# Two modulation gates summed on TensorE's column groups, and a fourth weight slot beside the attention

## The chip, the cores and the metric

The kernel runs on one core of a Trainium2 chip. The metric is the time of one execution in device microseconds, taken as the median of several runs. One further execution is taken with the hardware profiler; its rows are what this document reads. The engines are named as in the profile: PE is TensorE (PEld its weight loads), DVE is VectorE, ACT is ScalarE, POOL is GpSimd, and SP is SyncE, which issues most of the transfers.

## The reference, cut to what matters

Two transformer blocks run over 256 tokens of width 1024. The change lies in the first one, in the part that computes the modulation and the two attentions:

```
mod = (jax.nn.silu(c) @ w_ada + b_ada)[:, None, :]
sh_mix, sc_mix, g_mix, sh_ffn, sc_ffn, g_ffn = jnp.split(mod, 6, -1)
...
tiny = tiny_attention(tq, tk, tv, tk_c, tv_c) @ tiny_w_o
o_a = spatial_gating(u, v, tiny, sgu_ln_g, sgu_ln_b, sgu_w_s, sgu_b_s)
o_b = neighbourhood_attention(nq, nk, nv, nk_c, nv_c, na_rpb, rows)

merged = gate_a * (o_a @ w_up_a) + gate_b * (o_b @ w_up_b)
x = x + g_mix * (merged @ w_out)
```

`w_ada` is 1024 x 6144. Its six column blocks give shifts, scales and the two gates `g_mix` (block 2) and `g_ffn` (block 5), each a row of 1024 numbers. The neighbourhood attention has 16 heads and 256 queries over 512 keys (256 of the image, 256 of the context). After this part a mixture of 64 experts follows, and then the second block.

## The kernel before

All matrix products with large weights are made in three passes: a weight tile of 128 x 2048 numbers arrives through a ring of buffers (`Ring`, its transfer issued by SP on line 222), ACT writes its rounded part `whi` (line 352), DVE the remainder `wlo` (line 353), and TensorE runs three matmuls for each block (lines 392 to 394 in the function `fm`, called fm matmuls below). There are two pairs of `whi` and `wlo`. The ring has three lasting slots; other pools lend it more in some stages. A slot is given back when `whi` and `wlo` of its tile are written, or, for a tile of `w_ada`, when its sums are made. SP issues its transfers strictly in its own order, so one that waits for a slot holds those behind it.

The stage of this document lies at 157 to 281 us of the profile. Its main work is eight weight tiles of the gates `gate_a` and `gate_b` (384 fm matmuls that read `hh`). Woven into it is background work: first `sgu`, eight groups of four fp32 matmuls (lines 1245, 1246 and 1248; they contract over 64 rows, 1 row and 128 rows), whose operands `two`, `bs` and `wst` sit in the tile `tw`. Then comes `na`, the neighbourhood attention: four groups of heads `g`, two halves of the queries `q`, and in each two pairs of heads, 16 pairs in all. For a pair TensorE makes the scores (line 1311), DVE adds the bias table `T` (line 1320) and takes the maximum (line 1262), ACT takes the exponential (line 1265), TensorE transposes (line 1278) and ACT copies the result into the tile `PT` (line 1279). After two pairs `av` follows: the reciprocals of the four sums, spread over 32 columns each (line 1335), a matmul that transposes them (line 1337), the product with the values in four column groups of 32 (line 1344), and its scaling.

The two gates ride along in the same stage. `ada_sums` gives each gate four steps of one `w_ada` tile; a step is two instructions of DVE over 128 x 1024 numbers (line 749), which add the tile's rows, weighted by the SiLU of `c`, into the tile `gate_row`. Here they are partial sums in all 128 partitions. `gate_bcast` adds them up and spreads them by a matmul with ones (line 778) and copies the result out (line 779). The first two blocks of `w_ada` go another way, through `ada_group`: there TensorE makes the sums (line 701), with the 32 columns of `silp` as stationary operand and the tile's four stretches of 256 columns in the four column groups of the array.

A scheduler lays down the order of each engine's instructions when the program is built; on the chip each engine keeps that order.

Of the kernel before, what the change touches and what calls it, by code (L numbers as in the profile page):

```python
# [9 lines left out]
F32 = mybir.dt.float32  # L10
# [4 lines left out]
OP = mybir.AluOpType  # L15
# [256 lines left out]
class Kernel:  # L272
# [454 lines left out]
    def ada_sums(self, g):  # L727

        nc = self.nc
        st = {}  # L730

        def step(n):
            if n == 0:

                st["a"] = self.gate_row[g if g == 2 else 5]
                if g == 5:
                    self.gate_init(5)
            a = st["a"]
            i = self.i_ada[4 * self.ADA_ORDER.index(g) + n]
            w = self.ring.get(i)[:].rearrange("p (k c) -> p k c", k=2)  # L740

            j = min((j for j in self.lo_of if j > i), default=None)
            with self.tc.issue_after(self.lo_of[j].ins) if j else ExitStack():
                for k in range(2):
                    c = self.silp[:, 2 * n + k, 0:1]
                    if n == 0 and k == 0 and g in (3, 4):
                        nc.vector.tensor_scalar(a[:], w[:, k], c, None, op0=OP.mult)
                    else:
                        nc.vector.scalar_tensor_tensor(a[:], w[:, k], c, a[:], op0=OP.mult, op1=OP.add)
            self.ring.done(i)  # L750

        def end():
            if g in (2, 5):
                return
            st["ps"] = self.accp.tile([128, 512], F32, tag="acc", name="acc")

        def col(k):
            ps, a = st["ps"], st["a"]
            nc.tensor.matmul(ps[:, k:k + 1], a[:, k * 128:(k + 1) * 128], self.ones[:, 0:1], start=k == 0, stop=k == 7,
                             skip_group_check=True)  # L760
            if k == 7:
                c0 = V_AD + (g - 3) * 8
                nc.vector.tensor_tensor(self.mod[:, g, :, 0], ps[:, 0:8], self.vecs[:, c0:c0 + 8], op=OP.add)

        return [lambda n=n: step(n) for n in range(4)] + [end] + ([] if g in (2, 5) else [lambda k=k: col(k) for k in range(8)])

    def gate_init(self, g):
# [14 lines left out]
    def block1(self):  # L782
        tc, nc, A = self.tc, self.nc, self.A
# [115 lines left out]
        bg = []  # L899
        late = []  # L900
        for g in self.ADA_ORDER[2:]:
            a = self.ada_sums(g)
            if g == 4:
                bg += [late + a[0:1], a[1:2], a[2:3], a[3:4]]
            else:
                bg += [a[0:1], late + a[1:2], a[2:3], a[3:4]]
            late = a[4:]
        ada = bg

        def along(n):  # L910
# [97 lines left out]
        op, o_es = self.pool("op")  # L1008
        self.dump("nv", nv[:])


        tmp, tmp_es = self.pool("atmp", "right", bufs=2)
        oah = op.tile([128, 8, 256], F32R, name="oah")
        oal = Parts()
        obh = op.tile([128, 4, 256], F32R, name="obh")
        obl = op.tile([128, 4, 256], F32R, name="obl")
        bg = self.sgu(tmp, tT, u, v, oah, oal)
# [11 lines left out]
        self.weave(main, bg)  # L1029
        self.dump("oa", oah[:].bitcast(F32))  # L1030
        self.dump("ob", obh[:].bitcast(F32))
        tmp_es.close()
        att_es.close()
        xp, xp_es = self.pool("xp", "right")
# [196 lines left out]

    def sgu(self, tmp, tT, u, vn, oah, oal):
        nc, A = self.nc, self.A
        big = tmp.tile([128, 2048], F32, tag="PT", name="tw")
        two, bs, wst = big[0:64, 0:1024], big[64:65, 0:1024], big[:, 1024:2048]
        nc.sync.dma_start(two, A["two"])
        nc.sync.dma_start(bs, A["bs"])
        nc.sync.dma_start(wst, A["wst"])
        ones1 = self.ones[64:65, :]

        def sgu(g):
            ps = self.accp.tile([128, 512], F32, tag="acc", name="acc")
            o = ps[:, 0:256]
            gs = slice(g * 128, (g + 1) * 128)
            nc.tensor.matmul(o, two[:, gs], tT[:], start=True, stop=False, skip_group_check=True)
            nc.tensor.matmul(o, ones1, bs[:, None, gs].to_broadcast([1, 2, 128]), start=False, stop=False, skip_group_check=True)
            for n in range(2):
                nc.tensor.matmul(ps[:, n * 128:(n + 1) * 128], vn[:, n, gs], wst[:, gs], start=False, stop=n == 1,
                                 skip_group_check=True)
            nc.vector.tensor_tensor(o, u[g][:], o, op=OP.mult)  # L1250
            u[g] = None
            lo = self.up.tile([128, 256], F32R, tag="u", name="oal", bufs=9)
            oal.parts.append(lo)
            self.split(o, oah[:, g], lo[:])

        return [lambda g=g: sgu(g) for g in range(8)]
# [24 lines left out]
    def na(self, ap, tmp, qd, kd, nv, obh, obl):  # L1281
        nc, A, c = self.nc, self.A, self.c
        st = {}
# [40 lines left out]

        def trp(g, q, j):
            if j == 0:
                st["PT", g, q] = tmp.tile([128, 4, 4, 128], F32, tag="PT", name="PT")
            self.transposeP(st.pop(("p", g, q, j)), st["PT", g, q][:, :, j, :], 4)

        def av(g, q):  # L1330
            PT = st.pop(("PT", g, q))
            r = st.pop(("r", g, q))
            ps = self.accp.tile([128, 512], F32, tag="acc", name="acc")
            rB = tmp.tile([128, 4, 32], F32, tag="obf", name="rB")
            nc.vector.reciprocal(rB[:], r[:, :, None].to_broadcast([128, 4, 32]))

            nc.tensor.matmul(ps[:, 128:256], rB[:].rearrange("p a b -> p (a b)"), self.ident, start=True, stop=False,
                             skip_group_check=True)
            o = tmp.tile([128, 128], F32, tag="obf", name="o")
            nc.scalar.copy(o[:], ps[:, 128:256])  # L1340
            for k in range(4):
                for j in range(4):
                    h = 4 * g + j
                    nc.tensor.matmul(ps[32 * j:32 * j + 32, 0:128], nv[:, k, h * 32:(h + 1) * 32], PT[:, k, j, :],
                                     start=False, stop=k == 3, tile_position=(0, 32 * j), skip_group_check=True)
            nc.vector.tensor_tensor(o[:], ps[:, 0:128], o[:], op=OP.mult)
            s = slice(q * 128, (q + 1) * 128)
            b = self.vecs[:, V_BNV + g:V_BNV + g + 1]
            nc.scalar.activation(obh[:, g, s], o[:], AF.Identity, bias=b)
            nc.vector.scalar_tensor_tensor(obl[:, g, s], o[:], b, obh[:, g, s].bitcast(F32), op0=OP.add, op1=OP.subtract)  # L1350
# [5 lines left out]
        for n in range(len(items) + 1):  # L1356
            if n < len(items):
                g, q, j = it = items[n]
                if q == 1 and j == 0 and g < 3:
                    out.append(lambda g=g: load(g + 1))  # L1360
                if q == 0 and j == 0 and 0 < g < 3:
                    out.append(lambda g=g: stack(g + 1))
                out.append(lambda it=it: score2(*it))
            if n:
                g, q, j = items[n - 1]
                for jj in (j, j + 2):
                    out.append(lambda p=(g, q, jj): trp(*p))
                if j:
                    out.append(lambda g=g, q=q: av(g, q))
# [1031 lines left out]
```

## Time and profile before

| | |
|---|---|
| median of 3 runs | 1612.58 us (1611.51 to 1612.89) |
| the profiled execution | 1612.77 us |
| its span, first to last instruction | 1611.0 us |
| mean granted TensorE clock | 0.99 of full speed |
| TensorE, VectorE, ScalarE busy | 97%, 55%, 39% of the span |
| the stage with attention and gates | 157.55 to 281.24 us, 123.69 us |

The span is what the trace covers; 1.77 us of the profiled time lie around it. The granted clock is 1.00 at full speed (2.4 GHz) and 0.50 at half (1.2 GHz). A busy share says little by itself, since the stages of the kernel have different limits; below the stage is read by itself.

### The profile page before, as it was taken

What the parts mean: (1) busy time and instruction counts of PE and PEld (TensorE: products, weight loads), DVE (VectorE), ACT (ScalarE), POOL (GpSimd) and SP (SyncE); (2) the same over time, 40 slices, a digit from 0 to 9 for tenths busy, and PEclk for the clock granted to TensorE, in tenths of its full rate; (3) what the DMA queues carried; (4) which work ended last, traced back from release to release, by engine and by line L of the source; (5) the groups of instructions that cost most, each with busy time, mean ns of one, the idle gap of its engine ahead of it and who ended that gap; (6) DMA issues with size and microseconds to landing.
All of it is one profiled execution on the core that took longest, in us unless ns stands there. A gap on an engine that the chain in (4) does not pass through costs nothing. (4 is left out here: it accounts for less than half of the span.)

```text
span 1611.0 us, 26016 instructions
## 1 busy us (share of the span) xinstructions
PE 1557.7 (97%) x10509; PEld 1204.2 (75%) x10509; DVE 878.6 (55%) x1639; ACT 632.3 (39%) x1171; POOL 12.8 (1%) x23
## 2 busy tenths in 40 slices
PE   6999988999999999999989999999999999999997
PEld 4799876975443444443349999899999999899996
DVE  3696697663332323332344667964446565975453
ACT  3633366442111111111134756554433656644440
POOL 0000000000000000000000000000000000000000
PEclk9999999999999999999999999999999999999999
DMA  9788586878999999999955446565552444756530
GB/s 369 267 312 273 154 229 196 332 296 343 397 421 420 421 420 421 421 420 420 422 231 191 154 139 213 199 235 185 184 181 79 157 158 137 250 215 209 184 131 27
DMA packets 62972, 419.48 MB, mean 260 GB/s; under 512 B 7393, under 2 KB 9057, under 8 KB 14210
## 3 DMA queue, kind: packets, MB, share of 16 engines
q1 hardware_dynamic: 59010, 408.63, 67.7%
q0 software_dynamic: 1088, 5.61, 1.0%
q10 hardware_dynamic: 2752, 3.55, 0.6%
q8 instruction: 83, 1.36, 0.3%
q14 instruction: 39, 0.32, 0.1%
HBM read 413.05 MB, written 4.19 MB: 259 GB/s over the span
## 5 line engine op out<-in xcount | busy, mean ns | idle before, releaser
L353 DVE TENSOR_TENSOR wlo<-w,whi 128x1024 fp32r<-128x1024 f32 (+1 forms) x384 | 374.9, 1014 | 171.2 <-ACT whi L352 168.7
L352 ACT CAST whi<-w 128x1024 fp32r<-128x1024 f32 (+1 forms) x384 | 319.2, 883 | 316.9 <-PE mm L393 140.1
L392 PE MATMUL mm<-xTh,whi 128*128 128x256 f32 x960 | 274.5, 286 | 0.0
L394 PE MATMUL mm<-xTh,wlo 128*128 128x256 f32 x960 | 271.5, 283 | 0.0
L393 PE MATMUL mm<-xTl,whi 128*128 128x256 f32 x960 | 271.0, 282 | 0.0
L1627 PE MATMUL gu<-w,xg 128*64 128x512 f32 (+2 forms) x936 | 207.0, 596 | 0.0
L392 PEld LDWEIGHTS mm<-xTh,whi 128*128 128x128 f32 x960 | 182.9, 191 | 2.2 <-issue 1.4
L393 PEld LDWEIGHTS mm<-xTl,whi 128*128 128x128 f32 x960 | 183.4, 191 | 0.6
L394 PEld LDWEIGHTS mm<-xTh,wlo 128*128 128x128 f32 x960 | 182.8, 190 | 0.0
L1627 PEld LDWEIGHTS gu<-w,xg 128*64 128x64 f32 (+2 forms) x936 | 58.7, 127 | 98.5 <-issue 93.7
L1666 PE MATMUL y<-w,aT 128*64 128x512 f32 (+2 forms) x432 | 114.4, 599 | 0.0
L1648 DVE SCALAR_TENSOR_TENSOR sil<-sil,wsl,gu 128x256 f32<-128x256 f32 x26 | 12.5, 481 | 128.2 <-ACT sil L1647 127.6
L1764 ACT CAST yh<-yf 128x512 fp32r<-128x512 f32 x52 | 32.2, 619 | 125.9 <-DVE yf L1763 125.9
L392 PE MATMUL mm<-hh,whi 128*128 128x256 f32 x256 | 76.1, 299 | 5.6 <-ACT whi L352 3.9
L1763 DVE TENSOR_TENSOR yf<-y,gf 128x512 f32<-128x512 f32 x52 | 35.9, 690 | 79.4 <-PE y L1666 79.4
L394 PE MATMUL mm<-hh,wlo 128*128 128x256 f32 x256 | 75.0, 295 | 2.9 <-DVE wlo L353 2.9
L1666 PEld LDWEIGHTS y<-w,aT 128*64 128x64 f32 (+2 forms) x432 | 32.7, 126 | 57.5 <-issue 55.4
L393 PE MATMUL mm<-hl,whi 128*128 128x256 f32 x256 | 74.9, 294 | 0.3 <-DVE hl L289 0.3
L484 PE MATMUL acc<-whi,xTh 128*128 128x256 f32 x256 | 73.8, 289 | 0.0
L485 PE MATMUL acc<-wlo,xTh 128*128 128x256 f32 x256 | 72.6, 285 | 0.0
L486 PE MATMUL acc<-whi,xTl 128*128 128x256 f32 x256 | 72.4, 286 | 0.1
L1647 ACT ACTIVATE sil<-gu 128x256 f32<-128x256 f32 x26 | 10.0, 383 | 134.3 <-PE gu L1627 134.3
(449 smaller groups left out, 3119.9 us busy)
## 6 DMA issues: line engine op xcount, KB each, us to landing
w<-in_we SPq DMA_DIRECT2D x171, 1024.0 KB, 19.8
w<-in_w SPq DMA_DIRECT2D x156, 1024.0 KB, 4.9
w<-in_wada SPq DMA_DIRECT2D x23, 1024.0 KB, 8.9
wx<-in_we SPq DMA_DIRECT2D x21, 1024.0 KB, 19.8
ks<-kd SPq DMA_DIRECT2D x8, 512.0 KB, 7.3
lngb<-in_rows POOLq DMA_DIRECT2D x4, 1024.0 KB, 5.2
T<-in_rpb SPq DMA_DIRECT2D x8, 384.0 KB, 7.9
qs<-qd SPq DMA_DIRECT2D x16, 128.0 KB, 8.3
```

The costliest lines, as they stand in the source:

```text
L352: nc.scalar.copy(hi[:, s], w[:, s])
L353: self.lo_of[i] = nc.vector.tensor_tensor(lo[:, s], w[:, s], hi[:, s].bitcast(F32), op=OP.subtract)
L392: nc.tensor.matmul(ps, hi[:, k, mm], h, start=first, stop=False, skip_group_check=True)
L393: nc.tensor.matmul(ps, hi[:, k, mm], l, start=False, stop=False, skip_group_check=True)
L394: nc.tensor.matmul(ps, lo[:, k, mm], h, start=False, stop=last, skip_group_check=True)
L484: nc.tensor.matmul(o, h, wh, start=k == 0 and c % 2 == 0, stop=False, skip_group_check=True)
L485: nc.tensor.matmul(o, h, wl, start=False, stop=False, skip_group_check=True)
L486: nc.tensor.matmul(o, l, wh, start=False, stop=k == 7 and c % 2 == 1, skip_group_check=True)
L1627: nc.tensor.matmul(st["gu"][m * e:m * e + m, :], xg[:, k, s0:s0 + m], w[:, k % 4, :], start=k == 0, stop=k == 7, tile_position=(0, m * e))
L1666: nc.tensor.matmul(y[m * e:m * e + m, :], st["aT"][:, f * 128 + e * m:f * 128 + e * m + m], w[:, f, h * 512:(h + 1) * 512], start=f == 0, ...
L1763: nc.vector.tensor_tensor(t[0:n], y[0:n], g[0:n, h * 512:(h + 1) * 512], op=OP.mult)
L1764: nc.scalar.copy(yh[0:n], t[0:n])
```

## The change

1. For the two gates, `ada_sums` leaves DVE: each of the eight steps is now eight fp32 matmuls in four column groups of 32 (two rows of blocks `k`, four stretches `j` of 256 columns), all summing into one PSUM bank that is held over the gate's four steps. When a gate is done, DVE adds the first row of 256 to the bias row, and ACT copies the other three rows of 256 into partitions 32, 64 and 96 of `gate_row`. `gate_bcast` stays.
2. During the attention the ring has a fourth slot, `extn`, for tiles ahead of `w_up_a`. Its room comes from the tag `PT`, which `tw` and `PT` share and which has one buffer now instead of two.
3. The reciprocals in `av` are taken of the 128 x 4 sums, and a copy spreads them.

```diff
+            if g in (2, 5):
+                if n == 0:
+                    st["ps"] = self.mmp.tile([128, 512], F32, tag="mm", name="mm")
+                for k in range(2):
+                    for j in range(4):
+                        nc.tensor.matmul(st["ps"][32 * j:32 * j + 32, 0:256], self.silp[:, 2 * n + k, :],
+                                         w[:, k, j * 256:(j + 1) * 256], start=n == 0 and k == 0, stop=n == 3 and k == 1,
+                                         tile_position=(0, 32 * j))
+                self.ring.done(i)
+                return
...
             if g in (2, 5):
+
+                a, ps = st["a"], st["ps"]
+                nc.vector.tensor_tensor(a[0:1, 0:256], a[0:1, 0:256], ps[0:1, 0:256], op=OP.add)
+                for j in range(1, 4):
+                    nc.scalar.copy(a[32 * j:32 * j + 1, j * 256:(j + 1) * 256], ps[32 * j:32 * j + 1, 0:256])
                 return
...
+        bg[-1] = bg[-1] + late
         ada = bg
...
+        extn, extn_es = self.pool("extn", "right")
+        self.ring.open(extn, 1, self.i_upa[0])
...
-        big = tmp.tile([128, 2048], F32, tag="PT", name="tw")
+        big = tmp.tile([128, 2048], F32, tag="PT", name="tw", bufs=1)
...
-                st["PT", g, q] = tmp.tile([128, 4, 4, 128], F32, tag="PT", name="PT")
+                st["PT", g, q] = tmp.tile([128, 4, 4, 128], F32, tag="PT", name="PT", bufs=1)
...
-            nc.vector.reciprocal(rB[:], r[:, :, None].to_broadcast([128, 4, 32]))
+            nc.vector.reciprocal(r[:], r[:])
+            nc.vector.tensor_copy(rB[:], r[:, :, None].to_broadcast([128, 4, 32]))
```

The change also moves the order of the engines in this stage. Lines of the changed kernel are a little higher: its matmuls of `sgu` are on lines 1264, 1265 and 1267 (before 1245, 1246 and 1248), the scores on 1330, the transposes on 1297, the reciprocals' matmul on 1357, the values' on 1364, and `gate_bcast` on 793. The new gate matmuls are on line 746.

TensorE's order at a group of `sgu`, before; `acc` and `mm` are PSUM banks, `tT` the tiny attention's output:

```order
L394 MATMUL mm<-hh,wlo 128x256
L1245 MATMUL acc<-tT,tw 128x256
L1246 MATMUL acc<-tw,ones 128x256
L1248 MATMUL acc<-tw,v 128x128 x2
L392 MATMUL mm<-hh,whi 128x256
L393 MATMUL mm<-hl,whi 128x256
```

The same place in the changed kernel:

```order
L394 MATMUL mm<-hh,wlo 128x256
L1264 MATMUL acc<-tT,tw 128x256 x4
L1265 MATMUL acc<-tw,ones 128x256 x4
L1267 MATMUL acc<-tw,v 128x128 x8
L392 MATMUL mm<-hh,whi 128x256
L1264 MATMUL acc<-tT,tw 128x256
L1265 MATMUL acc<-tw,ones 128x256
L1267 MATMUL acc<-tw,v 128x128 x2
```

Before, five of the eight groups stand apart, with stretches of fm matmuls between them, and only the last three follow one another directly. Now all eight groups follow one another (the last three rows come four times) with a single fm matmul among them, and the 69 fm matmuls that stand ahead of them are preceded by the first gate step, eight matmuls on line 746.

SP's order at the transfers of `tw`, before (what a row waits for is in brackets):

```order
L222 DMA w<-in_wada 128x2048 [waits DMAHW2_49,DVE_49]
L1290 DMA ks<-kd_886 64x2048 [waits DMAHW3_49]
L1236 DMA tw<-in_two 64x1024 [waits DMAHW4_49,DVE_49]
L1237 DMA tw<-in_bs 1x1024 [waits DMAHW5_49]
L1238 DMA tw<-in_wst 128x1024 [waits DMAHW6_49]
L222 DMA w<-in_w 128x2048 [waits DMAHW7_49,DVE_49]
```

And in the changed kernel:

```order
L222 DMA w<-in_w 128x2048 [waits DMAHW5_49,DVE_49]
L222 DMA w<-in_wada 128x2048 [waits DMAHW6_49,PE_49]
L1255 DMA tw<-in_two 64x1024 [waits DMAHW7_49]
L1256 DMA tw<-in_bs 1x1024 [waits DMAHW0_49]
L1257 DMA tw<-in_wst 128x1024 [waits DMAHW1_49]
```

The transfers of `tw` now stand behind two more tiles of the ring, and the second of these waits for TensorE, for the first gate step.

TensorE's order at the end of the stage, before, from the last fm matmul that reads `hh` to the first that reads `oah`, the input of the next product:

```order
L394 MATMUL mm<-hh,wlo 128x256
L778 MATMUL mm<-gate_132,ones 128x512
L778 MATMUL mm<-gate_133,ones 128x512
L1278 MATMUL acc<-cst,P 128x128 x8
L1337 MATMUL acc<-cst,rB 128x128
L778 MATMUL mm<-gate_133,ones 128x512
L1344 MATMUL acc<-PT,nv 32x128 x16
L392 MATMUL mm<-oah,whi 128x256
```

And in the changed kernel:

```order
L394 MATMUL mm<-hh,wlo 128x256
L793 MATMUL mm<-gate_133,ones 128x512
L1297 MATMUL acc<-cst,P 128x128 x8
L1330 MATMUL acc<-ks,qs 128x512 x2
L1297 MATMUL acc<-cst,P 128x128 x8
L1357 MATMUL acc<-cst,rB 128x128
L1330 MATMUL acc<-ks,qs 128x512 x2
L1297 MATMUL acc<-cst,P 128x128 x4
L1364 MATMUL acc<-PT,nv 32x128 x16
L793 MATMUL mm<-gate_133,ones 128x512
L1297 MATMUL acc<-cst,P 128x128 x8
L392 MATMUL mm<-oah,whi 128x256
```

Before, one pair of heads is still to be transposed when the fm matmuls with `hh` are out; now it is the last four pairs, and 15 fm matmuls with `oah` stand ahead of the last product with the values. The 64 gate matmuls of line 746 stand in 13 runs: four steps whole, the other four cut by scores, transposes or fm matmuls.

## Rows read from the trace of the kernel before

**Rows 1.** Windows: stretch, PE, PEld, DVE, ACT, POOL busy (instructions), clock, DMA, GB/s.

```profile
157.55:281.24 123.69, 110.96 (x906) 91.59 (x905) 98.14 (x140) 69.70 (x157) 2.77 (x5) 0.94 0.65 187
281.24:440.00 158.76, 156.31 (x1023) 109.78 (x1023) 83.26 (x214) 50.85 (x96) 0.53 (x1) 1.00 0.87 341
```

**Rows 2.** TensorE's waits in 157.55 to 281.24: total us, times, longest.

```profile
PE mm L392 <- ACT whi L352: 3.4, 2, 1.9
PE mm L394 <- DVE wlo L353: 1.9, 3, 0.8
```

**Rows 3.** Windows of 0.5 and 5 us, columns as in rows 1.

```profile
175.00:175.50 0.50, 0.50 (x3) 0.16 (x1) 0.50 (x1) 0.21 (x1) 0.00 (x0) 0.65 0.19 37
181.50:182.00 0.50, 0.50 (x5) 0.50 (x4) 0.50 (x3) 0.00 (x0) 0.00 (x0) 0.53 0.00 0
...
175.00:180.00 5.00, 5.00 (x15) 3.13 (x14) 1.70 (x3) 0.58 (x2) 0.00 (x0) 0.51 0.65 222
180.00:185.00 5.00, 5.00 (x33) 4.83 (x32) 4.95 (x6) 0.37 (x1) 0.00 (x0) 0.80 0.16 21
230.00:235.00 5.00, 2.92 (x15) 2.66 (x16) 4.78 (x8) 4.50 (x9) 0.00 (x0) 0.82 1.09 228
235.00:240.00 5.00, 5.00 (x36) 4.77 (x35) 4.50 (x7) 3.05 (x8) 0.00 (x0) 0.84 0.96 264
260.00:265.00 5.00, 4.98 (x24) 3.87 (x24) 5.00 (x7) 5.00 (x11) 0.00 (x0) 0.66 0.32 77
```

**Rows 4.** Timeline of TensorE in `sgu`: start, us, instruction.

```profile
166.22 0.70 PE L1245 MATMUL acc<-tT,tw 64*128 64x256 f32 x2
167.93 0.36 PE L392 MATMUL mm<-hh,whi 128*128 128x256 f32 x1
...
171.92 0.28 PE L394 MATMUL mm<-hh,wlo 128*128 128x256 f32 x1
176.50 1.22 PE L1245 MATMUL acc<-tT,tw 64*128 64x256 f32 x2
179.66 0.56 PE L392 MATMUL mm<-hh,whi 128*128 128x256 f32 x1
```

**Rows 5.** Timeline of TensorE at line 701.

```profile
33.06 0.28 PE L393 MATMUL mm<-hl,whi 128*128 128x256 f32 x1
33.18 0.28 PE L394 MATMUL mm<-hh,wlo 128*128 128x256 f32 x1
33.39 1.07 PE L701 MATMUL acc<-w,silp 128*32 128x256 f32 x16
34.61 0.28 PE L393 MATMUL mm<-hl,whi 128*128 128x256 f32 x1
...
17.01 1.50 PE L701 MATMUL acc<-w,silp 128*32 128x256 f32 x24
```

**Rows 6.** Lines by form, 157.5 to 281.24, and two of the whole run.

```profile
L749 DVE SCALAR_TENSOR_TENSOR gate<-w,silp,gate 128x1024 f32<-128x1024 f32 x14 | 17.5, 1250 | 0.0
L1335 DVE RECIPROCAL rB<-rs 128x128 f32<-128x128 f32 x8 | 7.5, 942 | 1.2 <-ACT P L1265 1.2
...
L1656 DVE COPY aT<-misc 128x256 f32<-128x256 f32 x26 | 10.8, 417 | 0.2 <-PE misc L1654 0.2
L2263 DVE RECIPROCAL mnr<-mns 128x2 f32<-128x2 f32 x16 | 2.6, 161 | 6.9 <-ACT mb_p L2261 6.6
```

**Rows 7.** Timeline of TensorE: a pair's scores, and its first transposes.

```profile
236.24 0.79 PE L1311 MATMUL acc<-ks,qs 128*128 128x512 f32 x2
239.54 0.66 PE L1278 MATMUL acc<-cst,P 128*128 128x128 f32 x4
```

**Rows 8.** SP's timeline at `tw`, and the transfers view: us from issue to landing.

```profile
149.89 0.49 SPq L1236 DMA_DIRECT2D tw<-in_two  x1
159.09 0.35 SPq L222 DMA_DIRECT2D w<-in_w  x1
...
tw<-in_wst SPq DMA_DIRECT2D x1, 512.0 KB, 6.3
```

More of the change, by code (lines that the diff above doesn't have):

```diff
@@ L1031, in block1 @@
         self.dump("ob", obh[:].bitcast(F32))
+        extn_es.close()
         tmp_es.close()
```

## Prediction

> **What bounds the kernel now.** I read the stage of the change by itself first, in the windows. From its first fm matmul at 157.55 to the first matmul of the next product at 281.24 lie 123.69 us, in which TensorE is busy for 110.96, VectorE for 98.14 and ScalarE for 69.70 [rows 1]. The reader is to see two things: VectorE is the busiest engine beside TensorE, and TensorE has only 123.69 - 110.96 = 12.7 us of idle time for a relief of VectorE to give back. The stage's end matters in full, because in the stage behind it the transfers use 0.87 of the DMA engines' time while TensorE is busy for 156.31 of 158.76 us [rows 1]: nothing there could catch up what comes late, and a shift of the stage's end moves the kernel's end by as much.
>
> Next, the waits say what the idle time is: 3.4 + 1.9 = 5.3 us of it are waits for the two parts of a weight tile [rows 2]; the other 7.4 are links of the softmax chain (maximum, exponential, copies, reciprocals).
>
> Last, the clock. The mean granted clock of the stage is 0.94 [rows 1]. It is at half speed in three places. One is in `sgu`: windows of 5 us at 0.51 and 0.80 lose 5 x (0.49 + 0.20) = 3.45 us [rows 3]. The others follow the two longest weight waits: 0.82, 0.84 and 0.66 lose 5 x (0.18 + 0.16 + 0.34) = 3.4 us [rows 3]. Together 6.85 us.
>
> **Part 1, the gate sums on TensorE.** A step's shape stands in the trace, on line 701: 16 records (each fp32 matmul is recorded twice) are two blocks k, as one step needs. Between the fm matmuls that start at 33.18 and 34.61 stand one further fm start and the 16 records; fm matmuls follow each other by 33.18 - 33.06 = 0.12 us, so the step cost 1.43 - 0.24 = 1.19 us [rows 5]. A third block costs 1.50 - 1.07 = 0.43 us [rows 5], so two of them are 0.86, and 0.33 us are spent on going in and out. Eight steps are 9.5 us. They stand in 13 runs rather than 8, and five more times 0.33 is 1.7. Sum: **11.2 us more on TensorE**, the engine that sets the end. Bounds: 8 x 0.86 = 6.9 without any switch, 11.2 with all; I take the upper one, since the row shows the switch.
>
> The Trainium skill speaks against this change here: its page TensorEngine Tiling (Array Packing), under Tiling Modes, Key Properties, says that a change of the tiling mode drains TensorE. The 0.33 us agree with it; if switches were free, the forecast below would be 4.3 us lower.
>
> What it takes off VectorE: 16 instructions of 1.25 us, of which 14 (17.5 us) lie in the stage [rows 6]. What it adds there, two adds of one row of 256, is at most 0.42 each by the nearest row of that width [rows 6]; six copies of ScalarE are about as long, and hide on an engine that is idle for 54 us. The held PSUM bank is one of four where fm matmuls take one for each tile, so I cost it at nothing; were it missing, an evacuation would stand between two tiles.
>
> **Part 2, the small reciprocals.** Eight of 0.942 us become reciprocals of 128 x 4 (128 x 2 takes 0.161) and copies of 128 x 128 (between nothing and the 0.417 of 128 x 256; I take 0.28) [rows 6]: 8 x 0.5 = 4.0 us less on VectorE. With part 1 its work in the stage falls from 98.1 to 98.1 - 17.5 - 4.0 + 0.8 = 77.4 us. It is then no longer what TensorE waits for by sheer amount.
>
> **Part 3, the slot, and what the idle time becomes.** The fourth slot, and gate tiles that leave the ring as soon as TensorE reaches them, bring each weight tile a slot earlier. I let the 5.3 us of weight waits go, and with them the two falls of the clock behind them (3.4). Of the 7.4 us of chain waits I keep a quarter, 1.9: VectorE's queue is a fifth shorter, but the links stay. A new wait comes at the end, where the last four pairs now stand almost without fm matmuls between them. From a pair's scores to its first transposes the chain took 239.54 - 236.24 = 3.3 us [rows 7]; in the changed order only eight transposes, two scores and the reciprocals' matmul lie between (about 1.8 by the same rows), so TensorE waits some 1.5 us there, and at the two steps after it, where less stands between, about 1 us each: 3.5. Idle left: 1.9 + 3.5 = 5.4, given back: 12.7 - 5.4 = **7.3 us** (bounds 0 and 12.7). The 15 fm matmuls of the next product that now stand inside this end are done already: 15 x 0.12 = **1.8 us back**.
>
> The smaller buffer `PT` costs nothing, as TensorE's order puts each pair's transposes behind the product that reads the old contents, apart from three or four that start early. `tw` is the riskier one: SP issued it at 149.89, and the next weight tile at 159.09 [rows 8]; now it stands behind that tile and behind a gate tile that waits for the first gate step. That step ends at about 157.55 + 18 x 0.12 + 1.2 = 161, and 69 fm matmuls (8.3 us) lie between it and `sgu`; the transfer took 6.3 us [rows 8], behind two tiles now, so it is just in time, or late by up to 2 us. I take zero.
>
> **Part 4, `sgu` packed together.** A group takes 167.93 - 166.22 = 1.71 us at full clock [rows 4], eight of them 13.7. Five were interleaved with fm matmuls; the last three stood together, and in them the clock fell, at about 175.15 (0.65 as the mean of that half microsecond) [rows 3], 3.2 us after the last fm matmul had started at 171.92, with TensorE busy throughout; from then on the two records of line 1245 took 1.22 us instead of 0.70 [rows 4]. It rose at about 181.97 [rows 3], 2.3 us after fm matmuls came back at 179.66 [rows 4]. Now all eight stand together. I let the clock fall 4.5 us in (bounds 3.2, and 6): the other 13.7 - 4.5 = 9.2 us take twice as long, and the way back loses 2.3 / 2 = 1.15, together 10.35 us. Against the 6.85 us that the clock costs now, **3.5 us more**.
>
> **Sum:** + 11.2 - 7.3 - 1.8 + 3.5 = + 5.6 us on the profiled 1612.77 (1611.0 of span and 1.77 around it), 1618.4. The median shown, 1612.58, lies 0.2 lower, so I forecast **1618**.
>
> **Rivals.** (a) *The clock holds in the packed `sgu`.* Price: 10.35 us back, 1608, faster. For it: of the five groups between fm matmuls none lost the clock, and the new stretch has 69 fm matmuls ahead of it. Against it: the three groups that stood together did. It decides the sign if the clock costs less than about 1.5 us there. The Trainium skill's page TensorE: Matmul & The Clock Gate, section HAM oscillation, names idle gaps of TensorE as what takes the clock down, and by that rule it would hold here. The trace differs: the window at 175.00 is busy for 0.50 of 0.50 us as the clock falls.
> (b) *All idle time goes.* The 5.4 us that I leave vanish as well: 1613, no change. For it: VectorE at 77 of 124 us. Against: three engines (TensorE some 110, VectorE 77, ScalarE 70) must hand pairs on in a fixed order.
> (c) *The slot brings nothing.* SP's fixed order holds a weight tile behind a gate tile that waits for TensorE, the weight waits and both falls stay: 5.3 + 3.4 more, 1627. For it: exactly such a place at `tw`. Against: TensorE's gate steps stand well ahead of the tiles' turn.
>
> **How the numbers follow.** Chances: forecast 0.49 (1613 to 1625), (a) 0.28 (1603 if no idle time is left besides, to 1611), (b) 0.13, (c) 0.10. The whole range would be 1603 to 1627; 8 in 10 lie between 1604 and 1625, and the likeliest case alone in 1614 to 1624. A measurement of this kernel can tell some 0.2%, 3.2 us, from no change. Under 1609.4 lies nearly all of (a): 0.26 faster. Between lie (b), 0.04 of the forecast and 0.02 of (a): 0.19 the same. The rest, 0.55, is slower.
>
> **What the profile after would show.** Line 746 with 128 records in 13 runs, about 11 us of TensorE. One long fall of the clock in `sgu`, 16 us or more at half speed, and `na` starting some 8 us later than at 183. Behind it almost no wait of line 392 or 394 for `whi` or `wlo`, and no second fall. VectorE under 80 us in the stage. At the end three waits of TensorE for exponentials, about 3.5 us. From 157.55 to the last product with the values some 131 us, with the 15 `oah` matmuls already made in between. I am wrong if the clock stays at 1.00 through `sgu`, if a gate step takes clearly less than 1.2 us between fm matmuls, or if the idle time in `na` stays as it is.

## The result, and the profile after

The changed kernel takes 1623.1 us in the median of nine runs (1616.63 to 1628.5), against 1613.18 for the kernel before in nine runs. The ratio is 1.0055, interval 1.0043 to 1.0068: about 8.9 us slower (the two medians alone differ by 9.9). The profiled execution took 1624.43 us (span 1622.7). The nine runs differ by 12 us, and go with the granted clock of each: 0.984 in the two slowest (1628.5 and 1625.59), 0.986 to 0.987 in the middle four, 0.990 in the three fastest (1616.63 to 1618.03). The profiled execution of the kernel before has 0.990 too: so in the runs in which the clock loses no more than before, the change still costs some 3 to 5 us.

The windows of the stage after, from the first fm matmul that reads `hh` to the end of the last product with the values, whole and then cut where the clock changes (the last 4.7 us are at 1.00); the columns are those of [rows 1]:

```profile
157.20:295.40 138.20, 129.75 (x1049) 101.37 (x1048) 79.03 (x136) 72.36 (x163) 2.77 (x5) 0.89 0.62 179
157.20:174.20 17.00, 14.86 (x117) 13.34 (x117) 3.89 (x4) 3.66 (x7) 0.00 (x0) 1.00 0.89 240
174.20:198.20 24.00, 24.00 (x82) 15.61 (x80) 7.20 (x17) 4.81 (x10) 0.00 (x0) 0.50 0.37 83
198.20:269.70 71.50, 68.60 (x684) 55.35 (x676) 48.54 (x87) 46.12 (x110) 1.44 (x2) 1.00 0.70 203
269.70:273.70 4.00, 3.50 (x7) 1.79 (x7) 3.52 (x3) 2.35 (x3) 0.00 (x0) 0.57 0.57 215
273.70:286.70 13.00, 10.09 (x71) 8.38 (x70) 11.39 (x18) 8.30 (x19) 1.33 (x3) 1.00 0.53 182
286.70:290.70 4.00, 4.00 (x40) 2.81 (x39) 3.13 (x6) 3.25 (x9) 0.00 (x0) 0.57 0.00 0
```

The stage is 138.20 us long instead of 123.69 [rows 1]. TensorE is idle for 138.20 - 129.75 = 8.5 us (before 12.7). The clock, as busy time times what is missing to 1.00, loses 12.0 us in one stretch of 24 us at half speed and 1.5 and 1.7 in two short ones: 15.2 us (before 6.8, summed in the same way from windows of half a microsecond). What is left is TensorE's work at full speed: 129.75 - 15.2 - 1.8 for the 15 `oah` matmuls = 112.8, before 110.96 - 6.8 = 104.2. VectorE fell from 98.14 to 79.03 us, as forecast.

TensorE's timeline after, at the first gate step, in `sgu`, and at the last gate step:

```profile
159.33 0.28 PE L394 MATMUL mm<-hh,wlo 128*128 128x256 f32 x1
159.54 1.07 PE L746 MATMUL mm<-w,silp 128*32 128x256 f32 x16
160.54 0.39 PE L392 MATMUL mm<-hh,whi 128*128 128x256 f32 x1
160.76 0.28 PE L393 MATMUL mm<-hl,whi 128*128 128x256 f32 x1
...
168.79 0.28 PE L394 MATMUL mm<-hh,wlo 128*128 128x256 f32 x1
171.21 1.96 PE L1264 MATMUL acc<-tT,tw 64*128 64x256 f32 x8 [2.14 <-DMA tw<-in_two]
...
179.66 1.22 PE L1264 MATMUL acc<-tT,tw 64*128 64x256 f32 x2
...
183.10 1.22 PE L1264 MATMUL acc<-tT,tw 64*128 64x256 f32 x2
...
193.16 1.63 PE L1330 MATMUL acc<-ks,qs 128*128 128x512 f32 x3
194.59 0.41 PE L393 MATMUL mm<-hl,whi 128*128 128x256 f32 x1
...
266.36 1.06 PE L746 MATMUL mm<-w,silp 128*32 128x256 f32 x12
270.20 0.58 PE L392 MATMUL mm<-hh,whi 128*128 128x256 f32 x1 [2.78 <-ACT whi L352]
```

A whole gate step between fm matmuls costs 160.76 - 159.33 - 0.24 = 1.19 us, exactly the price read at line 701 [rows 5]. All gate matmuls together (128 records, in 13 runs; one step of them at half speed):

```profile
L746 PE MATMUL mm<-w,silp 128*32 128x256 f32 x128 | 11.8, 409 | 0.0
```

`sgu` waits 2.14 us for `tw`, then falls to half speed at 174.2, three microseconds in, and a group takes 183.10 - 179.66 = 3.44 us instead of the 1.71 of a group between fm matmuls [rows 4]. The clock is back at 198.2, 3.6 us after fm matmuls returned. At 267 TensorE stands still for 2.78 us behind its last gate step. The timeline of VectorE and ScalarE shows what happens there:

```profile
265.91 0.40 ACT L1369 ACTIVATE obh<-o,vecs 128x128 fp32r<-128x128 f32 x1 [1.67 <-DVE o L1366]
267.52 0.41 DVE L766 TENSOR_TENSOR gate<-gate,mm 1x256 f32<-1x256 f32 x1 [0.82 <-PE mm L746]
267.97 1.11 ACT L768 COPY gate<-mm 1x256 f32<-1x256 f32 x3 [1.65 <-DVE gate L766]
269.11 2.94 ACT L352 CAST whi<-w 128x1024 fp32r<-128x1024 f32 x3
```

The split of the last weight tile (line 352) stands in ScalarE's order behind the three copies of the second gate (line 768); they wait for VectorE's addition, and that for TensorE's gate step. So TensorE waits for itself, through two engines, while ScalarE stands idle twice for 1.7 us. TensorE's three largest waits in the stage (total, times, longest) follow. The first carries the names of an old weight wait [rows 2], but comes once, behind the copies of the gate; the others are new:

```profile
PE mm L392 <- ACT whi L352: 2.8, 1, 2.8
PE acc L1357 <- DVE rB L1355: 2.4, 2, 2.2
PE acc L1264 <- DMA tw<-in_two: 2.1, 1, 2.1
```

SP's timeline after, at `tw`, beside [rows 8]:

```profile
158.75 0.35 SPq L222 DMA_DIRECT2D w<-in_w  x1
160.67 0.35 SPq L222 DMA_DIRECT2D w<-in_wada  x1
161.07 0.49 SPq L1255 DMA_DIRECT2D tw<-in_two  x1
```

and from the transfers view, the us from issue to landing:

```profile
tw<-in_wst SPq DMA_DIRECT2D x1, 512.0 KB, 11.1
```

`tw` is issued at 161.07, not at 149.89, right behind the tile that waits for the first gate step, and takes 11.1 us to land instead of 6.3.

### The profile page after: what moved, and what is told of

Read it like the earlier page. It is cut to its first block, busy times and chain, and to the rows that moved or that the text cites. A ratio compares the mean times of both kernels' runs of the same rounds, so it can differ in the third digit from the quotient of the medians.

```text
span 1622.7 us, 26271 instructions
## 1 busy us (share of the span) xinstructions
PE 1575.0 (97%) x10637; PEld 1212.4 (75%) x10637; DVE 857.6 (53%) x1633; ACT 635.2 (39%) x1177; POOL 12.8 (1%) x23
```

## The experiments

Each ratio is to the kernel before, run beside it on the same chip; differences in us are (ratio - 1) x 1613. An interval reaches some 2 us to either side, so the difference of two rows is known to some 3 us. Idle and clock are of TensorE in the stage of the profiled execution, from its first fm matmul with `hh` to its last product with the values, worked out as above; in E8 to E11 3 to 38 of the fm matmuls with `hh` come behind that product.

| | gates | slot | `tw` by | ratio, interval | us | idle | clock |
|---|---|---|---|---|---|---|---|
| before | VectorE | 3 | SP | | | 12.7 | 6.8 |
| changed | TensorE | 4 | SP | 1.0055 [1.0043, 1.0068] | +8.9 | 8.5 | 15.2 |
| E1 | VectorE | 4 | SP | 0.9966 [0.9952, 0.9979] | -5.5 | 9.6 | 7.2 |
| E2 | TensorE | 3 | SP | 1.0043 [1.0029, 1.0057] | +6.9 | 11.4 | 8.5 |
| E3 | VectorE | 3 | SP | 0.9992 [0.9983, 1.0001] | -1.3 | 11.6 | 4.4 |
| E4 | VectorE | 4 | SP | 0.9973 [0.9961, 0.9985] | -4.4 | 10.0 | 7.4 |
| E5 | TensorE | 4 | POOL | 0.9994 [0.9985, 1.0003] | -1.0 | 5.0 | 1.5 |
| E6 | TensorE | 4 | POOL | 1.0004 [0.9990, 1.0018] | +0.6 | 4.5 | 13.1 |
| E7 | TensorE | 4 | SP | 1.0041 [1.0028, 1.0054] | +6.6 | 6.1 | 13.7 |
| E8 | VectorE | 4 | POOL | 0.9957 [0.9944, 0.9970] | -6.9 | 7.5 | 5.1 |
| E9 | TensorE | 4 | POOL | 0.9970 [0.9957, 0.9983] | -4.8 | 2.7 | 1.7 |
| E10 | VectorE | 3 | SP | 0.9980 [0.9966, 0.9994] | -3.2 | 10.0 | 5.1 |
| E11 | VectorE | 4 | POOL | 0.9940 [0.9927, 0.9954] | -9.7 | 6.5 | 3.3 |
| E12 | VectorE | 4 | POOL | 0.9963 [0.9950, 0.9977] | -6.0 | 8.4 | 5.1 |

**E1 to E4, the parts.** E1 takes the gate matmuls out of the changed kernel; E2, E3 and E4 put one part each into the kernel before.

```diff
E1 (to the changed kernel)
-            if g in (2, 5):
-                if n == 0:
-                    st["ps"] = self.mmp.tile([128, 512], F32, tag="mm", name="mm")
...
-                nc.vector.tensor_tensor(a[0:1, 0:256], a[0:1, 0:256], ps[0:1, 0:256], op=OP.add)
...
E2 (to before): these lines put in, with the change's line on `late`, and nothing else
E3 (to before)
-            nc.vector.reciprocal(rB[:], r[:, :, None].to_broadcast([128, 4, 32]))
+            nc.vector.reciprocal(r[:], r[:])
+            nc.vector.tensor_copy(rB[:], r[:, :, None].to_broadcast([128, 4, 32]))
E4 (to before)
+        self.ring.open(extn, 1, self.i_upa[0])
...
+        big = tmp.tile([128, 2048], F32, tag="PT", name="tw", bufs=1)
```

> The changed kernel with the gate sums back on VectorE: the fourth slot and the small reciprocals stay. TensorE's work is that of the kernel before; the eight groups of sgu stand as four and four with 36 fm matmuls between. My theory (the gate matmuls cost TensorE about 11 us and it sets the end): some 11 us less than the changed kernel, and less still if fewer groups together keep the clock; with part of the idle time given back, 1606 to 1611 against 1613 before. Rival (the price lies in the waits and the clock that the slot brings, not in the matmuls): it stays near 1620.

> The kernel before with the gate sums on TensorE alone: no fourth slot, reciprocals over 128 columns. My theory: the 64 matmuls cost about 11 us of TensorE, less what VectorE's relief gives back of the 12.7 us of idle time (a few us), plus a longer fall of the clock, since sgu is packed here as well (four groups, one fm matmul, four groups): 1620 to 1626. Rival (the matmuls fill idle time of TensorE, as VectorE is relieved by 17.5 us): 1613, no change.

> The kernel before with the small reciprocals alone. VectorE does 4 us less in the stage. My theory (VectorE's sum is not what TensorE waits for, but some links of the softmax chain go through the reciprocal): 0 to 1.5 us faster, 1611.5 to 1613. Rival (what VectorE is relieved of comes back in full): 4 us faster, 1609.

> The kernel before with the fourth slot alone, tw and PT sharing one buffer. My theory: the weight waits of 5.3 us and the clock falls of 3.4 us behind them go, while sgu stands as four and four groups and costs about as much clock as before: 1604 to 1609. Rival (the slot brings nothing, since SP's order holds the tiles behind others): 1613. Rival (one PT buffer makes the transposes wait for the product with the values): slower, 1616 or more.

All four medians (1609.15, 1621.25, 1611.97, 1608.2) lie where my theory put them. The small reciprocals can't be told from nothing. The stage windows of E1, and its two stretches of low clock:

```profile
157.64:280.01 122.37, 112.76 (x924) 93.75 (x924) 93.49 (x148) 70.11 (x157) 2.78 (x5) 0.93 0.68 201
...
178.64:185.64 7.00, 7.00 (x25) 5.35 (x25) 1.54 (x4) 0.75 (x2) 0.00 (x0) 0.51 0.60 223
263.64:274.64 11.00, 8.28 (x52) 5.81 (x53) 9.03 (x15) 8.18 (x20) 0.00 (x0) 0.53 0.49 166
```

and the stage of E2:

```profile
157.14:290.11 132.97, 121.56 (x1033) 96.01 (x1032) 82.84 (x128) 72.58 (x163) 2.77 (x5) 0.94 0.62 185
```

From these rows the gate matmuls have their price at full speed: the changed kernel's 112.8 less E1's 112.76 - 7.2 - 19 `oah` matmuls of 0.12 = 103.3 is 9.5 us; E2's 121.56 - 8.5 = 113.1 less 104.2 is 8.9. Such sums hold to some 2 us: without gate matmuls they give 104.2 before, but 105.3 in E3 (109.70 - 4.4) and 103.1 in E4 (112.38 - 7.4 - 1.9 for its 16 `oah` matmuls). VectorE's relief gives back only about 1.2 us of idle time, E1 to changed (9.6 to 8.5) as before to E2 (12.7 to 11.4), net of the waits that come with the gate matmuls. In E1 the second low stretch is the bare end of the stage and costs 8.28 x 0.47 = 3.9 us of clock. E4 has it too (266 to 274, 2.4 us); in E2, without the slot, it is shorter (286.6 to 290.1, 1.6 us).

But the parts do not add up: -4.4 + 6.9 - 1.3 = +1.2, and together they cost 8.9. Some 7.7 us, known to about 4, come from gates and slot meeting.

**E5 to E7, where they meet.**

```diff
E6 (to the changed kernel)
-        nc.sync.dma_start(two, A["two"])
-        nc.sync.dma_start(bs, A["bs"])
-        nc.sync.dma_start(wst, A["wst"])
+        nc.gpsimd.dma_start(two, A["two"])
+        nc.gpsimd.dma_start(bs, A["bs"])
+        nc.gpsimd.dma_start(wst, A["wst"])
E5: as E6, and
-        return [lambda g=g: sgu(g) for g in range(8)]
+        def held(g):
+            with self.tc.issue_after(self.last(mybir.EngineType.PE)):
+                sgu(g)
+        out = [lambda: None] * 5
+        for g in range(8):
+            out += [lambda g=g: held(g)] + [lambda: None] * 1
+        return out
E7 (to the changed kernel)
-        bg[-1] = bg[-1] + late
+        self.gate_end = late
...
         self.weave(main, bg)
+        for f in self.gate_end:
+            with self.tc.issue_after(self.lo_of[self.i_gb[-1]].ins):
+                f()
```

> The changed kernel, with tw's three transfers issued by POOL (past SP's queue), and the groups of sgu held apart by fm matmuls in TensorE's order (two together, then one at a time behind 6 or 12). The gate matmuls, the slot and the reciprocals stay. My theory (the whole surplus over the sum of the parts is the clock and the wait in sgu): the wait for tw (2.1 us) goes and the half speed in sgu costs under 3 us instead of 12: 1611 to 1615. Rival (gate matmuls and slot collide elsewhere: at the stage's end, or in the softmax chain): it stays at 1620 or more.

> The changed kernel with tw's transfers issued by POOL alone; TensorE's order still has all eight groups of sgu one after another (one fm matmul between), now behind 48 fm matmuls and without a wait. It tells the wait from the packing. My theory (the packing takes the clock down, as in the kernel before): the clock falls some 3 to 5 us into sgu all the same, its cost is 9 to 11 us instead of 12, and only the wait goes: 1617 to 1621. Rival (the 2.1 us in which TensorE stood still took the clock down): it stays at 1.00 through sgu, 1609 to 1612.

> The changed kernel with the last gate's addition and copies put behind the split of the last weight tile in the orders of VectorE and ScalarE; TensorE's order is word for word that of the changed kernel. My theory (the tile has long landed, and its split stands behind copies that wait for TensorE's last gate step): the 2.8 us wait of TensorE at 267 goes, with most of the fall of the clock behind it (2.4 us): 3 to 5 us less than the changed kernel, 1618 to 1620. Rival (the tile lands late): no change, 1623.

E6 gave 1612.13 where I expected 1617 to 1621. That is about the time of the rival (the wait took the clock down), but not for its reason, as the trace shows. Moving the three transfers of `tw` to POOL's queue, and what the scheduler makes of it, takes back 8.3 of the 8.9 us, with the gate matmuls in place and `sgu` packed as before. Its timeline of TensorE at the start of `sgu` and at the start of `na`, the gate matmuls, and the windows around the fall:

```profile
165.60 1.99 PE L1264 MATMUL acc<-tT,tw 64*128 64x256 f32 x8
...
189.69 1.71 PE L1330 MATMUL acc<-ks,qs 128*128 128x512 f32 x4
```

```profile
L746 PE MATMUL mm<-w,silp 128*32 128x256 f32 x128 | 9.4, 386 | 0.0
```

```profile
170.00:170.50 0.50, 0.50 (x7) 0.50 (x6) 0.31 (x1) 0.00 (x0) 0.00 (x0) 1.00 1.35 197
170.50:171.00 0.50, 0.50 (x5) 0.50 (x5) 0.48 (x2) 0.34 (x1) 0.00 (x0) 0.53 0.36 131
170.50:191.50 21.00, 21.00 (x66) 14.56 (x66) 8.99 (x20) 2.98 (x8) 0.00 (x0) 0.51 0.45 121
```

No wait stands ahead of `sgu`, TensorE is busy for every microsecond, and the clock falls all the same, 4.9 us in: in this run the packing takes it down, not the wait. Yet this profiled run (1615.36, clock 0.988) is one of twelve from 1605.46 (0.993) to 1618.33 (0.985): what the clock costs differs from run to run, and only this one has a trace. E5, with the groups apart, keeps full speed all through `sgu`, as its window there shows, and its eleven runs lie within 5.2 us:

```profile
166.50:187.50 21.00, 21.00 (x122) 15.42 (x121) 10.17 (x17) 7.69 (x15) 0.00 (x0) 1.00 0.63 174
```

But with a median of 1610.86 it is only 1.6 us better than E6 by the ratios, less than the two intervals can tell, although 11.6 us less of clock are lost in the profiled runs. E5's time lies just under the 1611 to 1615 that I expected, but after E6 it can't be put down to the clock. So of the surplus, what the move of `tw` gives, with the order that follows, is shown; the packing goes with times that spread over 13 us, and what it costs in the median stays open between nothing and some 4 us. E6's stage has 4.0 us less idle time (2.1 of it `tw`'s wait), and its `na` starts 3.5 us earlier (189.69 against 193.16). And not all of the gain is the queue's: the new order cuts the gate matmuls into 10 runs instead of 13, and line 746 is busy for 9.4 us instead of 11.8, of which a step at half speed explains some 0.6. How the 8.3 us divide between these I did not separate.

E7 leaves TensorE's order as it was. The 2.78 us wait is gone, as ScalarE's timeline there shows:

```profile
265.31 0.41 ACT L1372 ACTIVATE obh<-o,vecs 128x128 fp32r<-128x128 f32 x1 [1.67 <-DVE o L1369]
265.61 1.98 ACT L352 CAST whi<-w 128x1024 fp32r<-128x1024 f32 x2
269.39 1.12 ACT L768 COPY gate<-mm 1x256 f32<-1x256 f32 x3 [1.80 <-DVE gate L766]
```

The tile had landed: its split starts right behind the activation ahead of it, without a wait. The fall of the clock behind it is gone too (clock loss 15.2 to 13.7), the profiled time 1618.36; but the last wait of the stage grew from 2.2 to 2.9 us, and by the ratios the 2.3 us are within what the two intervals leave open. Right in its place, but 2.3 us where I expected 3 to 5.

**E8 to E12, repaired orders.** E12 is E1 with `tw` by POOL. E8 is E12 with one line changed; E11 is E8 with `sgu` held apart as in E5 (with one empty place ahead instead of five); E10 is the kernel before with the one line; E9 is the changed kernel with everything: E5, E7 and the line.

```diff
-        self.weave(main, bg)
+        self.weave(main, bg, 0.8)
```

> A version meant to beat both: slot and small reciprocals without the gate matmuls, tw's transfers issued by POOL, and the background spread over the first eight tenths of the fm matmuls, so that sgu's groups stand apart and the last pairs of heads have fm matmuls between them. My theory (what the slot gains is given back by the clock in sgu and by the bare end of the stage, together 8.5 us of clock in the kernel with the slot alone): 1600 to 1605. Rival (the idle time is the softmax chain's and only moves): about 1609, as with the slot and the reciprocals alone.

> The changed kernel with all three repairs: tw's transfers issued by POOL, sgu's groups held apart, the last gate's copies behind the split of the last weight tile, and the background spread over the first eight tenths of the fm matmuls. The gate matmuls stay. My theory (the gate matmuls' price of 9 to 10 us on TensorE is all that is left of the loss; what the slot and a covered stage end give is some 7 us, as in the version without the gate matmuls): 1612 to 1616 against 1613 before, that is 8 to 10 us above the version without them. Rival (with the stage's order repaired, VectorE's relief shows): 1605 or less.

> The kernel before with one number changed: the background is spread over the first eight tenths of the fm matmuls. No slot, no small reciprocals, no gate matmuls. It tells whether the gain of 6.9 us of the version without the gate matmuls needs the slot. My theory (the slot gave 4.4 us by itself, the covered end of the stage the rest): 1609 to 1612. Rival (the spread alone does it): 1606 to 1607.

> The version without the gate matmuls that was fastest so far, with sgu's groups also held apart one by one, behind 2, then 6 or 12 fm matmuls each. My theory: the fall of the clock in sgu (1.7 us) goes, 1 to 2 us less than without it, 1603 to 1605 where before is 1613. Rival (the clock falls elsewhere instead): no difference.

> The changed kernel with the gate sums on VectorE and tw's transfers issued by POOL. With the four kernels gates on TensorE or VectorE, tw by SP or by POOL, it tells whether tw's late place costs anything without the gate tile ahead of it. My theory (with the gates on TensorE the earlier transfers gave back 8 us; without them tw stands behind one tile less and sgu in two halves): at most 2 us less than with tw by SP, 1606 to 1608 where before is 1613. Rival (the place costs the same in both): 8 us less, 1600.

E12 against E1 is the fourth corner: without the gate matmuls the earlier `tw` gives 0.5 us (-5.5 to -6.0), with them 8.3 (+8.9 to +0.6). The late place by itself costs next to nothing; it costs together with the gate matmuls, and this difference, 7.8 us, is as large as the 7.7 by which the parts failed to add up (both known to about 4). How much of it is the late transfer itself, and how much the other order of the gate matmuls, these runs do not tell.

E9 refutes the rest of my theory. I expected the matmuls' 9 to 10 us to stay, 1612 to 1616; it takes 1606.63, some 5 us under the kernel before (2.7 to 6.9), and only 4.9 us above E11. My rival's 1605 or less it does not reach either. The stage of E9, and TensorE's longest waits in it:

```profile
157.25:269.95 112.70, 110.03 (x1007) 88.89 (x1006) 75.56 (x134) 66.36 (x154) 1.65 (x3) 0.98 0.64 192
```

```profile
PE mm L394 <- DVE wlo L353: 0.6, 2, 0.4
PE acc L1340 <- DVE o L1376: 0.5, 1, 0.5
```

The same of E11:

```profile
156.85:268.56 111.71, 105.24 (x896) 87.38 (x895) 90.97 (x146) 65.97 (x151) 1.66 (x3) 0.97 0.61 178
```

```profile
PE acc L1289 <- ACT P L1276: 2.3, 1, 2.3
PE acc L1349 <- DVE rB L1347: 1.9, 1, 1.9
```

With VectorE at 75.56 us TensorE is idle for 2.7 us in E9, against 6.5 in E11 with VectorE at 90.97: where no tile, transfer or copy stands in the way, 3.8 us of idle time come back, and 1.6 of clock. That pays for about half of the matmuls. That it is VectorE's relief fits E11's waits, which are for exponentials and reciprocals, but it is argued and not shown: the two kernels also differ in where the groups of `sgu` stand. E10 takes 1607.57, nearer to the rival (1606 to 1607) than to my 1609 to 1612: the one line is worth 3.2 us without slot or anything else. With the slot and the earlier `tw` (E12 to E8, which takes 1605.3 where I expected 1600 to 1605) it adds only 0.9, which the intervals can't tell from nothing. E11, without the gate matmuls, is the fastest: 1601.91 us, under the 1603 to 1605 that I expected and 9.7 below before.

## Why the prediction was near, and where it was off

The forecast was 1618, the median is 1623.1: the direction and the order of size were right, inside the range. The terms, against the profiled run (+11.66 us, 1.3 above its median):

| term | forecast | measured |
|---|---|---|
| gate matmuls | +11.2 | +8.9 and +9.5 (E2, E1), +8.6 in the stage's work |
| idle time, with the 15 `oah` matmuls that were to fill it | -9.1 | -4.3 |
| clock | +3.5 | +8.4 |
| sum | +5.6 | +12.7 in the stage |

The stage began 0.35 us earlier, and the remaining 0.7 us were made up behind it. Two terms missed by some 4.9 us each to the same side and the gate matmuls by 2.6 to the other, so the number is nearer than its terms, and part of that is luck. Of the signs that I named, the 128 records of line 746 in 13 runs, a gate step of 1.19 us and VectorE under 80 us came true. The old weight waits are gone, but line 392 waits once for `whi` for another reason; `na` started 10 us later than at 183, not 8, and the further falls of the clock that I had ruled out were there.

**The gate matmuls.** The mechanism and the price of a step (1.19 us) were right. The sums leave 1.7 to 2.6 us less than the 11.2, little more than what they hold to, and line 746 by itself is busy for 11.8; whether the five further runs cost less than 0.33 us each stays open. The Trainium skill's page TensorEngine Tiling (Array Packing), Tiling Modes, Key Properties, says that a change of the tiling mode drains TensorE. The whole step between fm matmuls agrees with it: 1.19 us against 0.86 for its matmuls alone [rows 5].

**The clock, the step that failed in size.** "I let the clock fall 4.5 us in", behind a `tw` that is "just in time": `tw` was 2.14 us late, just over the 2 us that I named as a bound and took as zero. The clock fell 3.0 us into `sgu`, the way back took 3.6 us instead of 2.3, with scores at half speed in it, and 24 us stood at half speed instead of some 21. And I let the weight waits go "and with them the two falls of the clock behind them", without asking whether the waits that I put in their place would bring their own: two did, 1.5 and 1.7 us, at 270 and at 287.

That `sgu` packed together takes the clock down without any idle time was right, and E6 shows it apart from the wait. The Trainium skill's page TensorE: Matmul & The Clock Gate, section HAM oscillation, names idle gaps of TensorE as what takes the clock down, and by that rule it would have held: the measurement decides against it here. Rival (a) falls with that in the profiled runs, though E6's fastest run, with a mean clock of 0.993 against 0.988, must have lost some 8 us less (an estimate, 0.005 x 1606).

**The idle time.** The weight waits of [rows 2] did go, and E4 shows that the slot is worth 4.4 us by itself (there line 392 waits 1.3 us for `whi`, line 394 no longer for `wlo`), so rival (c) is out. Of the 8.5 us of idle time, 2.14 are the wait for `tw` and 2.78 that behind the gate's copies; the other 3.5 are even less than the 5.4 that I kept. And the 1.8 us of the 15 `oah` matmuls should not have stood in the sum: they are work moved forward, which gains only where it fills idle time, and the 5.4 us were already all that I left; in the trace none of the 15 stands beside a wait. What came instead I had partly named (the bare end: 0.5, 0.2 and 2.25 us, 2.9 together against 3.5) and partly missed: I costed the copies on ScalarE at nothing, because it "is idle for 54 us". The idle time was there; the place in its order was not, and the wait went round three engines (2.78 us).

**What was missed most** is no term of the sum: that the place of `tw` costs far more than the wait for it. With its transfers on POOL's queue, and the order that follows (E6), the same change costs 0.6 us. I had named the place, "the riskier one", and priced only the wait. By which path the rest comes (`na` 3.5 us earlier, less idle time behind it, fewer cuts in the gate matmuls) stays open.

## What to carry to other kernels

When two parts of a change push on one queue, price their meeting, not each alone: here a slot (-4.4 us) and gate matmuls (+6.9) cost 8.9 together, with a small transfer behind the tiles of both, and moving its three DMA issues to an idle engine's queue, with the order that followed, gave 8.3 back. Work that is moved to hide on an engine with idle time must be followed to its place in that engine's order: what stands behind it there, and who waits for that. And a relief of an engine that is not the bound may pay only when the queues and orders around it are free (1.2 us of idle time here, 3.8 in the repaired order).

## What the runs showed of the hardware

TensorE's clock fell in a stretch in which the engine was busy without a gap: with groups of fp32 matmuls that contract over 64, 1 and 128 rows and next to no fm matmuls between, 3.0 us (before, changed) to some 6 us (E1) behind the start of the packed groups. With the groups one or two at a time between fm matmuls it stayed at 1.00 (E5, and E11 from 158 to 182). But packing does not settle it. In E3, where the same three groups stand together as before (there the third took 1.22 us for its first two records [rows 4]), they kept full speed to their end:

```profile
175.34 0.70 PE L1245 MATMUL acc<-tT,tw 64*128 64x256 f32 x2
176.59 0.71 PE L1248 MATMUL acc<-tw,v 128*128 128x128 f32 x4
```

And in E9, whose first three groups have only three and two fm matmuls among them, it fell 3.9 us behind their start:

```profile
168.00:172.00 4.00, 4.00 (x17) 3.30 (x18) 2.06 (x6) 1.12 (x3) 0.00 (x0) 0.57 0.81 284
```

The same order came out of this differently from run to run: the mean clock of the whole kernel was 0.985 to 0.993 in twelve runs of E6, and the time followed it, 1618.33 to 1605.46. At half speed a group of `sgu` took 3.44 us against (178.36 - 172.69) / 3 = 1.89 for packed groups at full speed in E1, 1.8 times and not twice:

```profile
172.69 0.70 PE L1249 MATMUL acc<-tT,tw 64*128 64x256 f32 x2
...
178.36 0.97 PE L1249 MATMUL acc<-tT,tw 64*128 64x256 f32 x2
```
